# Two feed-forward stages of a three-block forward pass: how the first and last block products are fed

## The chip, the cores and the metric

One core of a Trainium2 chip runs the whole program, from inputs in HBM to outputs in HBM. The metric is the device time of one execution in microseconds (us); the table below gives the median of three runs and a profiled execution.

## The reference

Three blocks with 1024 tokens of width 1024 run one after the other. The change touches the feed-forward part of the second and of the third:

```
# second block
x  = x + mix @ w_out
h2 = rms_norm(x, norm2_g)
x  = x + square(relu(h2 @ w_ff1)) @ w_ff2          # w_ff1 1024 x 4096, w_ff2 4096 x 1024
# third block
x  = x + concatenate([y_conv, y_mla]) @ w_o
hf = rmsnorm(x, norm_ffn_g)
a  = dwconv_centred(hf @ w_up, ffn_conv_w, ffn_conv_b)   # w_up 1024 x 5632, a convolution of 3 along the tokens
g, u = split(a, 2)
x  = x + (silu(g) * u) @ w_down                    # w_down 2816 x 1024
```

## The kernel before

**Tiles.** Activations lie with the channels on the 128 partitions: x[k][hf] is a tile of 128 channels by 512 tokens, k = 0..7, hf = ha or hb, the two halves of the tokens. Every fp32 operand is split by ACT and DVE into a rounded high part and the rest (hi by a cast on ACT, lo by a subtraction on DVE), and mm3 (L286, L287, L288) multiplies hi x hi, lo x hi and hi x lo, so that one 128 x 128 weight block against 512 tokens costs three matmuls.

**Block products.** Both stages save multiplications by Strassen's scheme in Winograd's form. blocks_of_input makes from the tokens the blocks 11, 21, 22 (in ffn3 also 12) and sums T1..T4 of them, each as four hi/lo pairs; some live in the pool tag S, the others in 24 tiles of tag E ("xe"). blocks_of_weights loads two rows of weights (wr), makes four sums S1..S4 in a tile "ss" (L372 to L375 on DVE), and split_w (L309 on ACT, L310 on DVE) makes four hi/lo weight sets, which live in a ring of 3 sets (wb) and nw more (wx; nw is 2 in ffn2 and 1 in ffn3). block_gemm runs seven products of 12 matmuls on them: 11, S1, S2, 12 x 21, S3, S4 and 22 x T4, and adds partial sums kept by ACT (L414) at the evictions. ffn2 has 16 such pairs, the first of them in another form (first_gemm, 9 products). ffn3 has 11 x 2, and the first two of these are plain products of 24 matmuls per half and part.

**ffn2** runs out_part (the output projection, which updates x) for ha, then for hb; each half is normed (squares, inverse_rms), split and spilled to DRAM (xf). The result of a pair goes through relu, a multiply with the norm's factor and a square (L1206, L1207), is summed into blocks again (L1214 to L1217) and stored to DRAM (hd). **ffn3** scales x in place (L1269), splits (L1259, L1260), runs the plain products, then a convolution (L1859 to L1861), a gate (L1286 to L1288) and the sums (L1295 to L1298), and stores.

**block_down** multiplies hd by the second weights in two groups of rows. It loads hidden blocks (hr, L1380) two at a time into a raw ring of two tiles, weight rows r1 (L1386) and r2 (L1394), and the spilled tokens x (L1231, L1361). It takes the seven sets in the order 11, 21, T1, T2, 22, T3, T4, makes the weight sums rs on the way, casts weight blocks to wph and wpl (L1438, L1439), and adds finished sets into x (L1448).

**Order.** Each engine runs its instructions in the order of a list that a scheduler makes when the kernel is built: it takes what is ready by a priority that follows the order of the code, and behind(by) puts a stretch of code that much later in it. Loads are all issued by SP and queue on one hardware queue over 16 DMA engines.

## Time and profile before

| | us |
|---|---|
| median of 3 runs (lowest to highest) | 3149.54 (3147.87 to 3151.3) |
| profiled execution, its own time | 3149.7 |
| its span, from the first to the last instruction | 3147.5 |
| TensorE busy in it | 3023.7 (96%) |
| VectorE (DVE) busy | 2329.6 (74%) |
| ScalarE (ACT) busy | 1419.5 (45%) |
| GpSimd (POOL) busy | 258.7 (8%) |
| mean granted TensorE clock | 0.984 |

The 2.2 us between span and time lie around the instructions. A matmul of 512 columns is recorded with some 0.39 us, but they overlap, so the rate is read from the number that start in a window. The granted clock is given as a share of full speed, 2.4 GHz; a stretch at the lower level, 1.2 GHz, has 0.5.

### The profile page before, as it was taken

The numbers are of one execution on the slowest core, as the hardware profiler recorded it, in microseconds if no ns is written. First come the engines' busy times: TensorE is split into PE (matmuls) and PEld (weight loads), VectorE is DVE, ScalarE is ACT, GpSimd is POOL, SyncE is SP. The second block draws the span as 40 slices with busy tenths as digits, with TensorE's granted clock in tenths as the row PEclk, the third lists the DMA queues.
The fourth block names the chain that finished last, engine by engine and source line by source line (L and its number), as shares of the span: only waits on it lengthen the run. The fifth ranks groups of instructions, "written<-read, shape, count | busy, mean of one in ns | idle before, by whom it ended". The sixth has DMA issues, their size and how long they took to land.

```text
span 3147.5 us, 40045 instructions
## 1 busy us (share of the span) xinstructions
PE 3023.7 (96%) x14472; PEld 2458.8 (78%) x14472; DVE 2329.6 (74%) x3633; ACT 1419.5 (45%) x2258; POOL 258.7 (8%) x352
## 2 busy tenths in 40 slices
PE   8999999999888999999899999999998999999998
PEld 6787888777666777888788888777776888878877
DVE  7756784858688888777867645577778888897776
ACT  3253463323366655444434443265644554454453
POOL 0011011213252000000000022000000000000000
PEclk9999999999999999999999999999999999999999
DMA  4241433423564334444743346642131323365232
GB/s 148 64 124 54 134 123 105 114 61 83 166 161 127 107 116 154 150 151 152 269 166 109 125 119 184 192 134 66 46 131 71 104 101 107 101 212 172 101 104 101
DMA packets 210751, 394.02 MB, mean 125 GB/s; under 512 B 31637, under 2 KB 71957, under 8 KB 210426
## 3 DMA queue, kind: packets, MB, share of 16 engines
q1 hardware_dynamic: 210554, 391.47, 39.5%
q8 instruction: 114, 1.87, 0.2%
q14 instruction: 83, 0.68, 0.1%
HBM read 272.78 MB, written 114.87 MB: 123 GB/s over the span
## 4 chain that ended last, share of the span: by engine, by line
PE 70%; DVE 8%; ACT 2%; issue 2%; DMA 2%; POOL 1%; SPq 0%; POOLq 0%; DVEq 0%; ACTq 0%
PE ps_G L286 12%; PE ps_G L287 12%; PE ps_G L288 12%; PE ps_g L286 4%; PE ps_g L287 4%; PE ps_g L288 4%; PE ps_o L1032 2%; PE ps_o L1033 2%; PE ps_t L2173 2%; PE ps_t L287 1%; PE ps_t L288 1%; PE ps_t L286 1%; PE ps_s L1645 1%; DVE se L1684 1%; PE ps_o L286 1%
## 5 line engine op out<-in xcount | busy, mean ns | idle before, releaser
L286 PE MATMUL ps_G<-xsh,wh 128*128 128x512 f32 (+1 forms) x1004 | 392.9, 391 | 19.0 <-ACT wh L309 11.1
L287 PE MATMUL ps_G<-xsl,wh 128*128 128x512 f32 (+1 forms) x1004 | 390.9, 390 | 1.6 <-DVE xsl L485 1.6
L288 PE MATMUL ps_G<-xsh,wl 128*128 128x512 f32 (+1 forms) x1004 | 390.7, 389 | 0.5 <-DVE wl L281 0.5
L280 ACT CAST wh<-wr 128x1024 fp32r<-128x1024 f32 (+1 forms) x147 | 150.1, 1022 | 272.9 <-PE ps_G L287 77.7
L286 PEld LDWEIGHTS ps_G<-xsh,wh 128*128 128x128 f32 x1004 | 190.2, 189 | 57.9 <-ACT wh L309 11.5
L281 DVE TENSOR_TENSOR wl<-wr,wh 128x1024 fp32r<-128x1024 f32 (+1 forms) x147 | 176.7, 1204 | 78.1 <-ACT wh L280 77.4
L287 PEld LDWEIGHTS ps_G<-xsl,wh 128*128 128x128 f32 x1004 | 189.8, 189 | 39.9 <-DVE xsl L485 2.8
L288 PEld LDWEIGHTS ps_G<-xsh,wl 128*128 128x128 f32 x1004 | 189.8, 189 | 39.1 <-DVE wl L281 1.2
L1031 DVE TENSOR_TENSOR ptl<-ps_t,pth 128x512 fp32r<-128x512 f32 (+3 forms) x288 | 168.6, 617 | 61.7 <-ACT pth L1030 60.2
L1030 ACT CAST pth<-ps_t 128x512 fp32r<-128x512 f32 (+3 forms) x288 | 142.7, 536 | 140.1 <-PE ps_t L2173 73.2
L286 PE MATMUL ps_g<-xsh,wh 128*128 128x512 f32 (+1 forms) x484 | 192.1, 397 | 3.0 <-DVE fa L1206 3.0
L287 PE MATMUL ps_g<-xsl,wh 128*128 128x512 f32 (+1 forms) x484 | 190.6, 394 | 0.3 <-DVE xsl L485 0.2
L288 PE MATMUL ps_g<-xsh,wl 128*128 128x512 f32 (+1 forms) x484 | 190.3, 393 | 0.0
L286 PE MATMUL ps_G<-xe,wh 128*128 128x512 f32 x448 | 176.2, 394 | 4.6 <-ACT xe L330 2.5
L287 PE MATMUL ps_G<-xe,wh 128*128 128x512 f32 x448 | 175.8, 392 | 0.1
L288 PE MATMUL ps_G<-xe,wl 128*128 128x512 f32 x448 | 175.5, 392 | 0.0
L286 PE MATMUL ps_G<-wh,wph 128*128 128x512 f32 x432 | 168.2, 389 | 0.7 <-ACT fz L1345 0.7
L287 PE MATMUL ps_G<-wl,wph 128*128 128x512 f32 x432 | 168.1, 389 | 0.0
L288 PE MATMUL ps_G<-wh,wpl 128*128 128x512 f32 x432 | 168.1, 389 | 0.0
L309 ACT CAST wh<-ss 128x1024 fp32r<-128x1024 f32 x70 | 73.4, 1050 | 151.2 <-PE ps_G L287 107.4
L310 DVE TENSOR_TENSOR wl<-hr,wh 128x1024 fp32r<-128x1024 f32 (+1 forms) x98 | 115.6, 1183 | 17.6 <-ACT wh L309 17.6
L1032 PE MATMUL ps_o<-pth,vst 128*128 128x512 f32 (+3 forms) x288 | 120.0, 417 | 8.8 <-ACT pth L1030 2.9
(618 smaller groups left out, 7603.7 us busy)
## 6 DMA issues: line engine op xcount, KB each, us to landing
wr<-in_w_in_dram SPq DMA_DIRECT2D x65, 512.0 KB
wr<-in_w_up_dram SPq DMA_DIRECT2D x44, 512.0 KB
wr<-in_w_ff_dram SPq DMA_DIRECT2D x33, 512.0 KB
r<-in_w_ff_dram SPq DMA_DIRECT2D x32, 512.0 KB
hr<-hT SPq DMA_DIRECT2D x32, 512.0 KB
h<-fa SPq DMA_DIRECT2D x48, 256.0 KB
hT<-ft SPq DMA_DIRECT2D x48, 256.0 KB
hr<-h SPq DMA_DIRECT2D x24, 512.0 KB
```

The lines of the kernel that those rows point to most:

```text
L280: nc.scalar.copy(hi[:, :n], raw[:, :n])
L281: nc.vector.tensor_tensor(lo[:, :n], raw[:, :n], hi[:, :n].bitcast(F32), op=ALU.subtract)
L286: mm(out, sh, mh, start=start, stop=False, **kw)
L287: mm(out, sh, ml, start=False, stop=False, **kw)
L288: mm(out, sl, mh, start=False, stop=stop, **kw)
L309: self.nc.scalar.copy(hi[:, c], z)
L310: self.nc.vector.tensor_tensor(lo[:, c], z, hi[:, c].bitcast(F32), op=ALU.subtract)
L1030: nc.scalar.copy(hi[:, c0:], tp[:, c0:])
L1031: nc.vector.tensor_tensor(lo[:, c0:], tp[:, c0:], hi[:, c0:].bitcast(F32), op=ALU.subtract)
L1032: nc.tensor.matmul(po[:, c0:], vs, hi[:, c0:], start=start, stop=False)
L1033: nc.tensor.matmul(po[:, c0:], vs, lo[:, c0:], start=False, stop=stop)
L2173: nc.tensor.transpose(tp[:, j * P:(j + 1) * P], pps[j][:, s * P:(s + 1) * P], self.ident)
```

## The change

- **blocks_of_input** is one function for both stages. It spills a half, norms it, scales the tokens in place (ffn2 by a multiply on ACT, ffn3 as before on DVE) and splits them in the order UPPER, then makes the sums T1..T4 in the place of the tokens (16 DVE additions) and splits these; block 12 is split as well. soon names T4 blocks that are split early. out_part goes through its output tiles in the order UPPER.
- **ffn2** computes its first two pairs with plain products (plain_gemm, 24 matmuls for each half and row of blocks) in place of first_gemm; the tiles fa move to a pool of their own, 13 instead of 8, and nw is 1 instead of 2.
- **The weight sums ss** lie in the pool fp, over rows of x that are freed when x is closed.
- **block_gemm** can take the product 12 x 21 second (early), which the first block pair of either stage does. The remaining T parts and the sums of the two plain pairs stand in behind(60), and in ffn3 also the finish of the second plain pair.
- **block_down** loads of the missing r1 rows two at once, into the tile of the weight sums (rr), and the rest, then x, then r2 two at a time between the loads of hr.

Cut to its core:

```diff
+UPPER = (4, 5, 6, 7, 0, 1, 2, 3)
...
-    def blocks_of_input(self, pool, extra, x, gain, a, b):
+    def blocks_of_input(self, pe, x, xf, nm, ha, hb, scale, soon=()):
...
+        B = {n: [None] * 4 for n in ("11", "12", "21", "22", "T1", "T2", "T3", "T4")}
+        new = lambda dt=F32: pe.tile([P, HF], dt, tag="E", bufs=24, name="xe")
+        def parts(n, k, hf):
+            src = x[k][hf]
+            hi, lo = (self.h("xs" + c, "S", F32R) for c in "hl") if n in ("11", "21", "22", "T1") else (new(F32R), new(F32R))
+            A.copy(hi, src)
+            V.tensor_tensor(lo, src, hi.bitcast(F32), op=ALU.subtract)
+            B[n][k % 4] = (hi, lo)
+        for hf, names in ((ha, ("11", "21")), (hb, ("12", "22"))):
+            self.spill(x, xf, hf)
+            _, nm.cols[hf] = self.inverse_rms(self.squares(new, [x[k][hf] for k in UPPER]), D, tag="n", bank="o")
+            for k in UPPER:
+                scale(k, hf)
+                parts(names[k // 4], k, hf)
+            yield B
         for k in range(4):
+            x11, x12, x21, x22 = x[k][ha], x[k][hb], x[k + 4][ha], x[k + 4][hb]
+            V.tensor_tensor(x22, x22, x12, op=ALU.subtract)
+            V.tensor_tensor(x12, x12, x11, op=ALU.subtract)
+            V.tensor_tensor(x11, x22, x11, op=ALU.add)
+            V.tensor_tensor(x21, x21, x11, op=ALU.subtract)
+        yield B
         for k in range(4):
+            parts("T1", k, hb)
+        for k in range(4):
+            parts("T2", k, ha)
+        for k in soon:
+            parts("T4", k, ha)
         yield B
+        for k in range(4, 8):
+            parts("T3", k, hb)
+        for k in range(4, 8):
+            if k not in soon:
+                parts("T4", k, ha)
         yield B
...
-    def blocks_of_weights(self, src1, src2, s):
...
+    def blocks_of_weights(self, src1, src2, pool):
...
-        s1, s2, s4, s3 = s if isinstance(s, list) else [s[:, i] for i in range(4)]
...
+        s = pool.tile([P, 4, HF], F32, tag="ss", bufs=1, name="ss")
+        V.tensor_tensor(s[:, 0], r2[:, lo], r2[:, hi], op=ALU.add)
+        V.tensor_tensor(s[:, 1], s[:, 0], r1[:, lo], op=ALU.subtract)
+        V.tensor_tensor(s[:, 2], r1[:, hi], s[:, 1], op=ALU.subtract)
+        V.tensor_tensor(s[:, 3], r1[:, lo], r2[:, lo], op=ALU.subtract)
+        f = s.rearrange("p n c -> p (n c)")
+        w1, w2, w3, w4 = (self.split_w(z) for z in (r1, f[:, :2 * HF], f[:, 2 * HF:], r2[:, hi]))
         cut = lambda w, c: (w[0][:, c], w[1][:, c])
         return {"11": cut(w1, lo), "12": cut(w1, hi), "22": w4, "S1": cut(w2, lo), "S2": cut(w2, hi), "S4": cut(w3, lo), "S3": cut(w3, hi)}
...
-    def block_gemm(self, pool, w, B, out):
...
+    def block_gemm(self, pool, w, B, out, early=False):
...
+        def first():
+            b = self.pt("g")
+            mul(b, w["12"], B["21"], True, True)
+            out("11", b, p1)
...
+        if early:
+            first()
...
-        u2 = self.keep(pool, "ku2", a)
-        b = self.pt("g")
-        mul(b, w["12"], B["21"], True, True)
-        out("11", b, p1)
+        u2 = keep(a, "ku2")
+        if not early:
+            first()
...
-    def first_gemm(self, w, B):
...
+    def plain_gemm(self, w, B, ha, hf, evict):
+        ps = self.pt("G")
+        self.block_product(ps, w, B["11"] + B["21"] if hf == ha else B["12"] + B["22"], True, True)
+        evict(ps)
...
-        with self.phase("f2", 2, G=4), tc.tile_pool(name="fe", bufs=1, reuse_waits="tile") as pe:
...
+        with self.phase("f2", 1, G=4), tc.tile_pool(name="fe", bufs=1, reuse_waits="tile") as pe, tc.tile_pool(name="fa", bufs=1, reuse_waits="tile") as pa:
+            def act(hf, ps, t=None):
+                z = pa.tile([P, HF], F32, tag="fa", bufs=13, name="fa")
+                if t is not None:
+                    V.tensor_tensor(z, ps, t, op=ALU.add)
+                V.scalar_tensor_tensor(z, ps if t is None else z, 0.0, nm.rst[hf], op0=ALU.max, op1=ALU.mult)
+                A.activation(z, z, AF.Square)
+                return z
...
+            def hidden(p, h):
...
+                V.tensor_tensor(h["12"], h["12"], h["11"], op=ALU.subtract)
+                V.tensor_tensor(t4, h["21"], t2, op=ALU.subtract)
+                for n, z in (("11", h["11"]), ("T1", h["12"]), ("21", h["21"]), ("T2", t2), ("22", h["22"]), ("T3", t3), ("T4", t4)):
+                    nc.sync.dma_start(hd[n][p], z)
+            steps = self.blocks_of_input(pe, x2, xf, nm, ha, hb, lambda k, hf: A.mul(x2[k][hf], x2[k][hf], self.v("norm2_g", k)))
...
+            def plain(p, hf):
+                for r in range(2):
+                    def ev(ps):
+                        h[p][f"{r + 1}{1 if hf == ha else 2}"] = act(hf, ps)
+                    self.plain_gemm(wts[p][r], B, ha, hf, ev)
+            for _ in self.out_part(w, xd, yt, x2, (5, 6, 7), (ha,)):
+                pass
+            B = next(steps)
+            for _ in self.out_part(w, xd, yt, x2, (5, 6, 7), (hb,)):
+                pass
+            wts = [[self.load_w(d["w_ff1"][p + 16 * r]) for r in range(2)] for p in range(2)]
+            plain(0, ha)
+            next(steps)
+            next(steps)
+            plain(0, hb)
+            plain(1, ha)
+            plain(1, hb)
+            next(steps)
+            with self.behind(60):
+                hidden(0, h[0])
                 next(steps)
+                hidden(1, h[1])
             self.close_x()
             self.fpool = tc.tile_pool(name="fp", bufs=1, side="right", reuse_waits="tile")
...
-                        wts = self.blocks_of_weights(d["w_ff1"][p], d["w_ff1"][p + 16], pf.tile([P, 4, HF], F32, tag="ss", bufs=1, name="ss"))
+                for p in range(2, 16):
+                    wts = self.blocks_of_weights(d["w_ff1"][p], d["w_ff1"][p + 16], fp)
...
-                        self.block_gemm(pf, wts, B, act)
...
+                    def out(n, ps, t):
+                        h[n] = act(ha if n[1] == "1" else hb, ps, t)
+                    self.block_gemm(pf, wts, B, out, p == 2)
+                    hidden(p, h)
...
+            def scale(k, hf):
+                V.scalar_tensor_tensor(x[k][hf], x[k][hf], self.v("norm_ffn_g", k), nm.rst[hf], op0=ALU.mult, op1=ALU.mult)
+            steps = self.blocks_of_input(pe, x, xf, nm, ha, hb, scale, (7,))
...
+            def plain(j, hf):
+                for part in range(2):
+                    self.plain_gemm(wts[j][part], B, ha, hf, lambda ps: A.copy(z[j][part][:, zs(hf)], ps))
...
-            split_half(ha, ("11", "21"))
+            B = next(steps)
...
-            for part in range(2):
-                plain(wts[0][part], ha, z[0][part])
-            split_half(hb, ("12", "22"))
...
+            plain(0, ha)
+            next(steps)
+            next(steps)
+            plain(0, hb)
+            h = [finish(0, z[0]), None]
...
-                for part in range(2):
-                    plain(wts[1][part], hf, z[1][part])
-            h[1] = finish(nf, z[1])
-            for n, o, hf in (("T1", 0, hb), ("T2", 0, ha), ("T3", 4, hb), ("T4", 4, ha)):
-                for k in range(4):
...
+            plain(1, ha)
+            plain(1, hb)
+            next(steps)
+            with self.behind(60):
+                next(steps)
+                h[1] = finish(nf, z[1])
...
-                        wts = self.blocks_of_weights(d["w_up"][f], d["w_up"][22 + f], p2.tile([P, 4, HF], F32, tag="ss", bufs=1, name="ss"))
+                        wts = self.blocks_of_weights(d["w_up"][f], d["w_up"][22 + f], fp)
...
-                        self.block_gemm(p2, wts, B, out)
+                        self.block_gemm(p2, wts, B, out, f == 1)
+                        if f == 1:
+                            with self.behind(60):
+                                blocks(0, *h, p2)
...
-                    blocks(i, *h, p2)
+                    if i:
+                        blocks(i, *h, p2)
...
+            def load_r1(kk):
+                for k in kk:
+                    o = ks.index(k)
+                    if o < nfp:
+                        r1[k] = fp.tile([P, 2 * HF], F32, tag="r1", bufs=nfp, name="r1")
+                    elif o == nfp:
+                        both = fp.tile([P, 4, HF], F32, tag="ss", bufs=1, name="rr").rearrange("p n c -> p (n c)")
+                        r1[k] = both[:, :2 * HF]
+                        if o + 1 < len(ks):
+                            r1[ks[o + 1]] = both[:, 2 * HF:]
+                    elif o > nfp + 1:
+                        r1[k] = pd.tile([P, 2 * HF], F32, tag="r1", bufs=nb - nfp - 2, name="r1")
+                    nc.sync.dma_start(r1[k], rows(k))
...
-            for o, k in enumerate(ks):
-                if k not in r1:
-                    r1[k] = (fp if o < nb // 2 else pd).tile([P, 2 * HF], F32, tag="r1", bufs=nb // 2, name="r1")
-                    nc.sync.dma_start(r1[k], rows(k))
+            need = [k for k in ks if k not in r1]
+            two = [ks[j:j + 2] for j in range(0, len(ks), 2)]
+            n1 = 2 if load_x is not None else len(need)
+            load_r1(need[:n1])
...
-                load_x(0, ha)
...
+                later += [lambda: load_r1(need[n1:]), lambda f=load_x: f(0, ha)]
+            later += [lambda kk=kk: load_r2(kk) for kk in two]
...
-        for n in range(KT):
+        for n in UPPER:
```

Three places of the order, first before, then after (the lines are those of each kernel). DVE at the start of ffn3, when the second half's tokens are scaled: vn ends the norm, x is scaled by the norm's factor rst, xe and xsl are the low parts; x_18165, x_18515, x_18871, x_19221 are tiles 0 to 3 before, and x_18128, x_18478, x_18834, x_19184, x_19540 are tiles 4, 5, 6, 7 and 0 after.

```order
L507 TENSOR_SCALAR vn_21252<-ps_o_21247 128x4
L1269 SCALAR_TENSOR_TENSOR x_18165<-x_18165,vc_70,rst_21256 128x512
L1269 SCALAR_TENSOR_TENSOR x_18515<-x_18515,vc_70,rst_21256 128x512
L1269 SCALAR_TENSOR_TENSOR x_18871<-x_18871,vc_70,rst_21256 128x512
L1260 TENSOR_TENSOR xe_21265<-x_18165,xe_21264 128x512
L1269 SCALAR_TENSOR_TENSOR x_19221<-x_19221,vc_70,rst_21256 128x512
L1260 TENSOR_TENSOR xe_21270<-x_18515,xe_21269 128x512
```

```order
L489 TENSOR_SCALAR vn_21215<-ps_o_21210 128x4
L1244 SCALAR_TENSOR_TENSOR x_18128<-x_18128,vc_70,rst_21219 128x512
L1244 SCALAR_TENSOR_TENSOR x_18478<-x_18478,vc_70,rst_21219 128x512
L1244 SCALAR_TENSOR_TENSOR x_18834<-x_18834,vc_70,rst_21219 128x512
L327 TENSOR_TENSOR xsl_21228<-x_18128,xsh_21227 128x512
L1244 SCALAR_TENSOR_TENSOR x_19184<-x_19184,vc_70,rst_21219 128x512
L327 TENSOR_TENSOR xsl_21233<-x_18478,xsh_21232 128x512
L1244 SCALAR_TENSOR_TENSOR x_19540<-x_19540,vc_70,rst_21219 128x512
```

Tile 0, the first of block 12, was scaled first and is now scaled fifth.

DVE before the first block pair of ffn3: fc, fth and ft belong to the convolution, the gate and the block sums of the plain pairs, xe to the T parts, ss are the weight sums.

```order
L1287 SCALAR_TENSOR_TENSOR fth_21509<-fth_21509,fc_21497 128x512
L1260 TENSOR_TENSOR xe_21562<-x_19579,xe_21561 128x512
L1288 SCALAR_TENSOR_TENSOR fc_21501<-fth_21509,fc_21501 128x512
L1260 TENSOR_TENSOR xe_21566<-x_19929,xe_21565 128x512
L1260 TENSOR_TENSOR xe_21570<-x_20285,xe_21569 128x512
L1260 TENSOR_TENSOR xe_21574<-x_20674,xe_21573 128x512
L1295 TENSOR_TENSOR ft_21584<-fc_21501,fc_21381 128x512
L372 TENSOR_TENSOR ss_21598<-wr_21600 128x512
L1296 TENSOR_TENSOR ft_21585<-ft_21584,fc_21381 128x512
L1297 TENSOR_TENSOR fc_21381<-fc_21381 128x512
L1298 TENSOR_TENSOR ft_21586<-fc_21501,ft_21585 128x512
L373 TENSOR_TENSOR ss_21598<-ss_21598,wr_21599 128x512
```

```order
L1841 SCALAR_TENSOR_TENSOR fc_21524<-fz_21350,vc_70,fc_21524 128x1024
L327 TENSOR_TENSOR xe_21513<-x_18130,xe_21512 128x512
L1842 SCALAR_TENSOR_TENSOR fc_21524<-fz_21350,vc_70,fc_21524 128x1024
L327 TENSOR_TENSOR xe_21517<-x_18480,xe_21516 128x512
L308 TENSOR_TENSOR wl_21569<-wr_21548,wh_21568 128x512
L327 TENSOR_TENSOR xe_21521<-x_18836,xe_21520 128x512
L366 TENSOR_TENSOR ss_21551<-wr_21548 128x512
L369 TENSOR_TENSOR ss_21551<-wr_21547,wr_21548 128x512
L367 TENSOR_TENSOR ss_21551<-ss_21551,wr_21547 128x512
L1841 SCALAR_TENSOR_TENSOR fc_21528<-fz_21353,vc_70,fc_21528 128x1024
L368 TENSOR_TENSOR ss_21551<-wr_21547,ss_21551 128x512
```

The gate and the block sums that stood between the T parts and the second weight sum are gone from there, and the weight sums follow the T parts.

SP at the step from ffn2's pairs to its down product: h and hT are stores of the hidden blocks, r are weight rows (L1386 and L1362 for r1, L1394 and L1367 for r2), x the spilled tokens, hr the hidden blocks.

```order
L1386 DMA r_13665<-in_w_ff_dram 128x1024
L1231 DMA x<-xf 128x512 x4
L1394 DMA r_13679<-in_w_ff_dram 128x1024
L1394 DMA r_13682<-in_w_ff_dram 128x1024
L1394 DMA r_13721<-in_w_ff_dram 128x1024
L1394 DMA r_13724<-in_w_ff_dram 128x1024
L1394 DMA r_13765<-in_w_ff_dram 128x1024
L1394 DMA r_13768<-in_w_ff_dram 128x1024
L1394 DMA r_13809<-in_w_ff_dram 128x1024
L1394 DMA r_13812<-in_w_ff_dram 128x1024
L1380 DMA hr<-h_10761 128x2x512
L1231 DMA x<-xf 128x512 x4
```

```order
L1362 DMA r_13633<-in_w_ff_dram 128x1024
L1367 DMA r_13717<-in_w_ff_dram 128x1024
L1221 DMA x<-xf 128x512 x4
L1367 DMA r_13720<-in_w_ff_dram 128x1024
L1367 DMA r_13761<-in_w_ff_dram 128x1024
L1367 DMA r_13764<-in_w_ff_dram 128x1024
L1347 DMA hr<-h_10761 128x2x512
L1367 DMA r_13813<-in_w_ff_dram 128x1024
L1367 DMA r_13816<-in_w_ff_dram 128x1024
L1347 DMA hr<-h_10761 128x2x512
L1367 DMA r_13857<-in_w_ff_dram 128x1024
L1367 DMA r_13860<-in_w_ff_dram 128x1024
```

The first hr of block 21 stood behind eight r2 loads and stands behind four now, and x between the first two of them.

## Rows read from the trace of the kernel before

**Rows 1.** TensorE, 100 us: width, busy (starts) by engine, clock, DMA share, GB/s.

```profile
1500.00:1600.00 100.00, 89.16 (x382) 72.77 (x381) 76.87 (x110) 42.84 (x62) 0.00 (x0) 0.93 0.67 236
...
2600.00:2700.00 100.00, 100.00 (x443) 82.81 (x442) 89.17 (x110) 50.51 (x64) 1.27 (x20) 1.00 0.32 106
```

**Rows 2.** TensorE's waits over the execution: total us, times, longest.

```profile
PE ps_g L286 <- ACT wh L309: 15.1, 2, 8.9
...
PE ps_G L286 <- ACT wh L309: 11.1, 1, 11.1
...
PE ps_g L286 <- DVE fa L1206: 3.0, 1, 3.0
...
PE ps_G L286 <- ACT xe L330: 2.5, 1, 2.5
...
PE ps_g L287 <- DVE wl L310: 2.4, 2, 1.9
...
PE ps_G L286 <- ACT xe L1259: 2.1, 1, 2.1
...
PE ps_o L522 <- POOL un L510: 1.5, 2, 1.3
```

**Rows 3.** Short windows around the waits, columns as in rows 1.

```profile
1192.00:1208.00 16.00, 10.30 (x30) 6.82 (x29) 15.32 (x24) 8.68 (x15) 0.00 (x0) 0.68 0.53 180
1512.00:1532.00 20.00, 9.16 (x29) 6.57 (x28) 20.00 (x33) 12.07 (x19) 0.00 (x0) 0.66 0.96 352
2360.00:2372.00 12.00, 8.55 (x37) 6.81 (x36) 7.58 (x13) 4.89 (x8) 1.01 (x1) 0.86 0.00 0
2404.00:2424.00 20.00, 8.91 (x31) 6.73 (x31) 18.68 (x28) 8.16 (x13) 0.13 (x2) 0.74 0.59 210
2820.00:2836.00 16.00, 9.39 (x32) 6.82 (x31) 15.84 (x25) 10.11 (x16) 0.00 (x0) 0.79 0.73 266
```

**Rows 4.** ACT and DVE at ffn2's start: start, us, engine, line, operation.

```profile
1195.41 3.26 ACT L330 CAST xe<-bt 128x512 fp32r<-128x512 f32 x6 [3.31 <-DVE bt L354]
...
1197.94 2.49 DVE L331 TENSOR_TENSOR xe<-bt,xe 128x512 fp32r<-128x512 f32 x4
1200.35 0.68 DVE L1206 SCALAR_TENSOR_TENSOR fa<-ps_g,rst 128x512 f32<-128x512 f32 x1
```

**Rows 5.** Timeline of SP, ACT, DVE from ffn2 to down; one window.

```profile
1503.07 6.90 SPq L1394 DMA_DIRECT2D r<-in_w_ff_dram  x8
1510.92 0.38 SPq L1380 DMA_DIRECT2D hr<-h  x1
...
1521.48 1.04 ACT L309 CAST wh<-hr 128x1024 fp32r<-128x1024 f32 x1
...
1513.48 2.47 DVE L1448 TENSOR_TENSOR x<-x,ps_G 128x512 f32<-128x512 f32 x4
...
1508.00:1516.00 8.00, 5.68 (x26) 4.36 (x24) 5.37 (x10) 2.48 (x4) 0.00 (x0) 1.00 1.03 412
```

**Rows 6.** Timeline of ACT at ffn3's start.

```profile
2365.37 1.94 ACT L1259 CAST xe<-x 128x512 fp32r<-128x512 f32 x3 [0.82 <-DVE x L1269]
...
2369.22 0.62 ACT L1259 CAST xsh<-x 128x512 fp32r<-128x512 f32 x1 [0.64 <-DVE x L1269]
```

**Rows 7.** Timeline of DVE, ACT, TensorE before ffn3's first block pair.

```profile
2405.08 1.28 DVE L1861 SCALAR_TENSOR_TENSOR fc<-fz,vc,fc 128x1024 f32<-128x1024 f32 x1
...
2415.31 0.68 DVE L373 TENSOR_TENSOR ss<-ss,wr 128x512 f32<-128x512 f32 x1
...
2416.03 1.04 ACT L309 CAST wh<-ss 128x1024 fp32r<-128x1024 f32 x1 [5.25 <-DVE ss L373]
...
2417.12 0.80 PE L286 MATMUL ps_G<-xsh,wh 128*128 128x512 f32 x1 [11.09 <-ACT wh L309]
```

**Rows 8.** Timeline of SP and ACT from ffn3 to down.

```profile
2820.87 0.37 SPq L1380 DMA_DIRECT2D hr<-g  x1
...
2827.96 1.04 ACT L309 CAST wh<-hr 128x1024 fp32r<-128x1024 f32 x1 [2.73 <-DMA hr<-g]
```

196 lines of the change are left out of this document (33 added, 163 removed).

## The prediction

> **What bounds the kernel now.** First the table of 100 us windows [rows 1]. In an undisturbed stretch (2600-2700) TensorE is busy 100% at granted clock 1.00 and starts 443 matmuls in 100 us, 0.2257 us each; the window 1500-1600 has 89.16% and 382. TensorE's issue is the bound, so time is to be gained only where it stands still or runs at the lower clock. Then TensorE's waits over the whole execution [rows 2], of which seven are in the diff's reach, and short windows around them [rows 3]. A window's loss is its width less its matmuls times 0.2257: start of ffn2 16 - 30 x 0.2257 = 9.2 us (A); from ffn2's pairs to its down product 20 - 6.5 = 13.5 (B); first block pair of ffn3 20 - 7.0 = 13.0 (C); from ffn3's pairs to its down product 16 - 7.2 = 8.8 (D). At the start of ffn3 (C0) the window also holds twelve short matmuls of the norm, so I add instead: waits of 1.3 (POOL's un) and 2.1 us (xe, L1259), and 12 x 0.14 x 2 = 3.4 us at half clock, of which half is lost: 5.1 us. Together **49.6 us**: no fix of these five places can bring more, so 3149.7 - 49.6 = 3100.1 us is the floor.
>
> The two levels are 1.2 and 2.4 GHz, so clock means of 0.68, 0.66, 0.86, 0.74 and 0.79 [rows 3] are 10.2 + 13.6 + 3.4 + 10.4 + 6.7 = 44.3 us at the lower. The waits themselves are 5.5 + 10.8 + 3.4 + 11.1 + 6.6 = 37.4 us [rows 2], so the clock costs 49.6 - 37.4 = 12.2. The Trainium skill (TensorE: Matmul & The Clock Gate, section HAM oscillation) reckons the loss as half of the throttled time, here an estimate of 22.2 us, and 59.6 in all. The trace does not agree: TensorE stood still for much of the throttled time, and the counts of matmuls leave 12.2. By that rule the sum below would grow by 59.6/49.6 (rival 6).
>
> **No work is added for TensorE.** ffn2 had 9 products of 12 matmuls in its first pair and 15 x 7 after: 114. Two plain pairs are 2 x 8, and 14 x 7 remain: 114. ffn3 keeps its two plain pairs. Each edit therefore moves only what TensorE waits for.
>
> **A, start of ffn2.** Before, the scaled T sums are made while TensorE is already at the products that need them: ACT's casts of the parts wait 3.31 us for a sum (L354) and begin at 1195.41, DVE makes the last four low parts from 1197.94, and only then the eviction L1206 at 1200.35, for which TensorE waits [rows 4]. That piece gives the unit costs too: 0.6 us for a DVE part (four in 2.49), 0.54 for an ACT cast (six in 3.26). After, the two plain pairs need only parts of 11, 21, 12, 22: 192 matmuls x 0.2257 = 43.3 us of cover. Under it DVE has 8 low parts of hb, 16 in-place sums, 16 T parts, 4 weight sums (44 x 0.6 = 26.4), 8 evictions (5.4) and 4 weight splits (4.8): 37 us. ACT has 16 multiplies or casts of hb, 16 T casts, 8 + 8 squares (48 x 0.6 = 29) and 4 weight casts (4.2): 33 us. Both fit, DVE by 6 us. The order puts the T4 parts, which need the E tiles of 12 free, and the first weight sums behind the fourth eviction pair; the cast of S1, S2 then follows TensorE's last read of 12 by some 2.7 + 4 x 0.6 us, and TensorE needs it two products (5.4 us) after the plain pairs. Where the multiply in place waits for its spill to land, ACT holds all casts behind it; a slip of the whole 9.2 us is needed to lose it all. Gain **9.2**, bounds 4 and 9.2: DVE 5 us over its cover leaves 5. The weight ring falls from 5 sets to 4; ffn3 has run with 4 before, at 100% in 2600-2700 [rows 1], so it is costed at nothing.
>
> **C0, start of ffn3.** The tokens are now scaled 4..7, 0..3, so 12's first block, which TensorE's first matmul of plain(0, hb) needs, is the fifth instead of the first. Before, the first cast begins at 2365.37 and the fifth at 2369.22 [rows 6]: **3.85 us** later. The stand-still grows from 2.1 to 6.0 us, and with it, I take it, the stretch at half clock from 3.4 to 6.8 us, 1.7 more. Cost 3.9 to 5.6.
>
> **C, first block pair of ffn3.** Before, DVE reaches L373 at 2415.31, ACT's cast follows at 2416.03, TensorE goes on at 2417.12 [rows 7] and pays 13.0 - 11.1 = 1.9 us more for the low clock, as if it went on at full speed from 2419.0. In the order of before 25 DVE rows follow the 1024-wide split of wr up to and with L373; after, 16. Two convolution steps (1.2 each: L1861), four gate steps and four output sums (8 x 0.6) less, one more weight sum: 6.6 us, and up to 1.8 us of waits between them. Thus L373's end falls from 2416.0 to 2407.6-2409.4, the cast ends a microsecond later, at 2408.6-2410.5. TensorE itself, which ran out of work at 2417.12 - 11.09 = 2406.0 and is moved by C0, arrives at 2409.9-2411.6. So it hardly waits, and C0 and C together gain 2419.0 - 2410.7 = 8.3; 0.8 off for the split of the lows: **7.5**, bounds 4 (a wait of 3 us is left, and its clock) and 10.4 (C0 costs nothing; then DVE is the bound, 2419.0 - 2408.6). The 6.6 us of DVE work moved behind must fit into the block pair that follows (7 x 12 x 0.2257 = 19 us); only the pairs' stores to hd wait for it.
>
> **B, ffn2 to down.** Before, the loads of r2 (8 x 0.524 MB) are issued from 1503.07, hr of block 21 behind them at 1510.92, and its cast begins at 1521.48; the engines move 412 GB/s there [rows 5]: they are full, and the queue's order decides. After, four r2 stand behind hr and two r1 go out before the last stores, into free time: 6 x 0.524 / 0.412 = 7.6 us earlier, the cast at 1513.9, and ACT has four r2 casts fewer ahead of it. TensorE is due at 1521.48 + 1.1 - 8.9 = 1513.7. The two early r1 go into the weight-sum tile and wait on SP until pair 15's splits have read it, with three hr of 11 and the pair's stores queued behind them; those hr are needed before 1513.7 as well, but 11 was fed without a wait before. But the low part (DVE, 1.2 us) now stands behind the additions into x, which wait for product 11 to end and take 2.47 for four [rows 5]; one of them is ahead: 0.6 + 1.2 us. I take a wait of 1.8 and 1.7 of clock: gain 13.5 - 3.5 = **10**, bounds 6 (hr 4 us later) and 13.5.
>
> **D, ffn3 to down.** hr of 21 goes from behind twelve x loads (12 x 0.262 MB = 3.1 MB) to before them: 3.1 / 0.412 = 7.6 us, cast at 2827.96 - 7.6 = 2820.4 [rows 8], due at 2827.96 + 1.1 - 6.2 = 2822.9. Hidden. The x loads land later by one hr (1.3 us), and x is added to at the end of 11, with the low part behind it on DVE: gain **8.5**, bounds 5 and 8.8. Behind these DMAs the SP queue holds the next hr alone, which waits for a ring slot anyhow.
>
> The second group of either down product, and the end phase, keep their loads; a few matmuls trade places: 0, bounds -3 and +3.
>
> **Sum.** 9.2 + 7.5 + 10 + 8.5 = 35.2 us off the profiled execution of 3149.7 us (span 3147.5 and 2.2 around it), which is 0.2 over the median of the runs. **3114.5 us.**
>
> **Rivals.** (1) *The loads stay late*: with the engines full, stores and x compete with hr and B and D bring half. For it: 412 GB/s at 1508-1516 [rows 5]. Against: In 1500-1600 the queue alone delays hr. B 5, D 4: 3124. (2) *The backlog moves*: DVE is over its cover in A (5 left) and C keeps 5: 3125. For it: DVE was at the parts until 1200.35 [rows 4]. (3) *Everything goes*: UPPER costs nothing, the low part of B is in time: 9.2 + 10.4 + 13.5 + 8.8 = 41.9, 3108. Against: the scale waits for the norm, which comes at the same time. (4) *Slower, by the weight ring of ffn2*: with 4 sets a pair's last set is recast only after the pair before has read it; if that cast and split (1.05 + 1.2 us) stood once in each of 14 pairs, with 1.7 of clock, it is 4 x 14 = 56 us: 3114.5 + 56 = 3170. It outweighs the gain from 35.2 / 14 = 2.5 us a pair. Against: ffn3 at 100% with the same ring [rows 1]. (5) *It doesn't do what it says*: hr, S1 and the plain pairs wait nearly as long for what stands next in line (x additions, E tiles, spills), and 5 us of the 35 remain: 3145. (6) *The clock gives back more than its rows*: half of the 44.3 us, so 35.2 x 59.6 / 49.6 = 42: 3107.
>
> **How the numbers follow.** Forecast 0.48, (1) 0.18, (2) 0.15, (3) 0.05, (6) 0.02, (5) 0.06, (4) 0.06. A measurement here tells 0.2%, 6.3 us, from no change: faster below 3143.2. Faster 0.88, same 0.06, slower 0.06. The forecast's own bounds are about 3108 and 3122. The range leaves out (4) and (5), reaches below (3) and (6), and above (1) and (2) to where both come half together: 3104 to 3132.
>
> **What would show it.** Right: no wait on L1206 or xe at ffn2's start; TensorE's wait on the first xe of ffn3 near 6 us instead of 2.1; L309's waits of 11.1, 8.9 and 6.2 gone or under 2; the windows of 1500-1600 and 2800-2900 at 98% or more; 14 pairs of ffn2 at 100%. Wrong: waits on wh or wl in each pair of ffn2 (4); a wait on hr's cast above 4 us (1); DVE without idle and TensorE waiting on ss or xe (2).

## The result and the profile after

The changed kernel takes 3115.46 us (median of four runs, 3111.93 to 3118.55) against 3148.70 (3147.56 to 3151.30) for the kernel before beside it: ratio 0.9893, interval 0.9881 to 0.9906. The forecast was 3114.5, with a range of 3104 to 3132. The profiled execution took 3116.86 us, with a span of 3115.1; the span of before is 3147.5.

The 32.4 us between the spans (33.2 between the medians; 35.2 were forecast) can be laid to stretches, by cutting both traces at the same instructions: the first matmul of ffn2's down product, the norm's column sums behind it, those at the start of ffn3, the first matmul of ffn3's down product, and its end.

| stretch | before | after | gained | forecast |
|---|---|---|---|---|
| start to ffn2's down product (A) | 1491.73 | 1487.79 | 3.94 | 9.2 |
| ffn2's down product to the norm (B) | 318.56 | 305.15 | 13.41 | 10 |
| attention | 520.83 | 519.56 | 1.27 | 0 |
| start of ffn3 to its down product (C0, C) | 464.25 | 457.40 | 6.85 | 7.5 |
| ffn3's down product (D) | 218.16 | 209.96 | 8.20 | 8.5 |
| end | 134.01 | 135.21 | -1.20 | 0 |

So the sum came out within 2.8 us, C and D did, and two terms missed in opposite directions: A by 5.3 us, B by 3.4.

The windows of 100 us, in the columns of [rows 1]: ffn2's start, its pairs, its step to down, and the end of ffn3's step to down, which now begins at 2769.90.

```profile
1100.00:1200.00 100.00, 94.40 (x443) 75.33 (x442) 77.03 (x124) 59.15 (x101) 8.41 (x2) 0.98 0.36 112
...
1300.00:1400.00 100.00, 100.00 (x443) 82.87 (x442) 68.57 (x98) 40.48 (x57) 0.00 (x0) 1.00 0.47 161
...
1500.00:1600.00 100.00, 99.78 (x440) 82.35 (x439) 84.44 (x123) 46.20 (x67) 0.00 (x0) 1.00 0.73 257
...
2800.00:2900.00 100.00, 99.30 (x439) 82.03 (x438) 84.90 (x122) 44.41 (x64) 0.00 (x0) 1.00 0.49 162
```

The window that began at 1500 stood at 89.16% and 382 matmuls [rows 1]; it is full now. The pairs of ffn2 run at 443 matmuls in 100 us with four sets of weights: rival 4 is refuted by that row. TensorE's waits, as [rows 2] (total, times, longest), of the places in the diff's reach:

```profile
PE ps_G L287 <- ACT xe L326: 6.0, 1, 6.0
PE ps_o L504 <- POOL un L492: 4.5, 3, 3.0
...
PE ps_g L287 <- DVE x L1429: 0.7, 1, 0.7
PE ps_G L289 <- DVE wl L308: 0.6, 1, 0.6
```

The line that was L309 (the cast of a weight, 15.1 and 11.1 us) is L307 now and is not among the waits at all; nor is the eviction fa. The wait on the first xe of ffn3 is 6.0 us in the place of 2.1, as forecast. What was not forecast is the second line: un, which cost 1.5 us in all, costs 4.5, with one wait of 3.0. Both are seen in short windows, columns as before:

```profile
1184.00:1200.00 16.00, 13.04 (x53) 10.40 (x52) 11.00 (x20) 5.49 (x9) 7.40 (x1) 0.89 0.04 16
...
2340.00:2360.00 20.00, 12.52 (x51) 9.54 (x50) 14.22 (x24) 7.37 (x12) 1.01 (x1) 0.74 0.02 8
```

**A, the new wait.** POOL is busy for 7.40 us with one instruction of 128x4 in the first window. The timelines of POOL, DVE and TensorE there (start, length, engine, line; x are the in-place sums):

```profile
1184.23 7.40 POOL L492 TENSOR_TENSOR un<-vn,nhalf 128x4 f32<-128x4 f32 x1 [23.61 <-DVE vn L489]
...
1183.99 0.15 DVE L489 TENSOR_SCALAR vn<-ps_o 128x4 f32<-128x4 f32 x1
1184.06 0.69 DVE L339 TENSOR_TENSOR x<-x 128x512 f32<-128x512 f32 x1
...
1190.08 0.69 DVE L340 TENSOR_TENSOR x<-x 128x512 f32<-128x512 f32 x1
...
1191.69 0.73 PE L504 MATMUL ps_o<-cn,un 128*128 128x128 f32 x4 [2.96 <-POOL un L492]
```

vn is there at 1184.14; un begins at once and ends at 1191.63, 0.86 us after the last of the in-place sums with which the change fills DVE. TensorE, which needs un for the norm's rows, stands still for 2.96 us, and the granted clock of the window is 0.89: 16 x 0.11 x 2 = 3.5 us at the lower level behind it. In the kernel before, the same instruction took 1.38 us:

```profile
1175.77 1.38 POOL L510 TENSOR_TENSOR un<-vn,nhalf 128x4 f32<-128x4 f32 x1 [16.43 <-DVE vn L507]
```

**B.** ACT and DVE at the step to down, the rows that answer to [rows 5]:

```profile
1507.79 1.05 ACT L307 CAST wh<-hr 128x1024 fp32r<-128x1024 f32 x1 [0.80 <-DMA hr<-h]
...
1507.71 0.69 DVE L1429 TENSOR_TENSOR x<-x,ps_G 128x512 f32<-128x512 f32 x1
1508.87 1.23 DVE L308 TENSOR_TENSOR wl<-hr,wh 128x1024 fp32r<-128x1024 f32 x1 [0.48 <-ACT wh L307]
```

Counted from the down product's first matmul, the cast of block 21 comes at 20.0 us in the place of 29.75: 9.75 us earlier, where 7.6 were forecast. Only one addition into x stands ahead of the low part, and it was over by then; the forecast wait of 1.8 us is not there, only 0.22 us for the low part itself.

**C and D.** Of the first block pair of ffn3, DVE's sum, ACT's cast and TensorE (compare [rows 7]):

```profile
2390.00 0.68 DVE L367 TENSOR_TENSOR ss<-ss,wr 128x512 f32<-128x512 f32 x1
...
2390.72 1.05 ACT L307 CAST wh<-ss 128x1024 fp32r<-128x1024 f32 x1 [0.43 <-DVE ss L367]
...
2393.68 0.50 PE L289 MATMUL ps_G<-xsh,wl 128*128 128x512 f32 x1 [0.61 <-DVE wl L308]
```

The cast ends at 2391.77 and TensorE comes to it at 2392.0, without a wait where 11.09 us stood; 0.61 is left for the low part. In D the cast of block 21's last rows, the one that TensorE waited for before, comes 2791.73 - 2769.90 = 21.8 us behind the first matmul, in the place of 32.6 [rows 8]: 10.8 us earlier, where 7.6 were forecast. Behind it 0.70 us of waits remain, for an addition into x:

```profile
2791.73 1.04 ACT L307 CAST wh<-hr 128x1024 fp32r<-128x1024 f32 x1
...
2803.53 0.47 PE L287 MATMUL ps_g<-wh,wph 128*128 128x512 f32 x1 [0.70 <-DVE x L1429]
```

### The profile page after: what moved, and what is told of

Same layout as the page of the kernel before. It is cut to its first block, busy times and chain, and to the rows that moved or that the text cites. A ratio compares the mean times of both kernels' runs of the same rounds, so it can differ in the third digit from the quotient of the medians.

```text
span 3115.1 us, 39929 instructions
## 1 busy us (share of the span) xinstructions
PE 3018.5 (97%) x14472; PEld 2457.3 (79%) x14472; DVE 2310.0 (74%) x3618; ACT 1420.2 (46%) x2263; POOL 264.4 (8%) x352
## 4 chain that ended last, share of the span: by engine, by line
PE 70%; DVE 8%; issue 2%; ACT 2%; DMA 2%; POOL 1%; SPq 0%; POOLq 0%; DVEq 0%; ACTq 0%
PE ps_G L287 12%; PE ps_G L288 12%; PE ps_G L289 12%; PE ps_g L287 4%; PE ps_g L288 4%; PE ps_g L289 4%; PE ps_o L1014 2%; PE ps_o L1015 2%; PE ps_t L2154 2%; PE ps_t L287 1%; PE ps_t L289 1%; DVE se L1665 1%; PE ps_t L288 1%; PE ps_s L1626 1%; PE ps_o L287 1%
## 5 line engine op out<-in xcount | busy, mean ns | idle before, releaser
L287 PE MATMUL ps_G<-xsh,wh 128*128 128x512 f32 (+1 forms) x1024 | 400.8, 391 | 8.3 <-ACT xsh L462 6.4
L288 PE MATMUL ps_G<-xsl,wh 128*128 128x512 f32 (+1 forms) x1024 | 399.1, 390 | 1.0 <-DVE xsl L467 1.0
L289 PE MATMUL ps_G<-xsh,wl 128*128 128x512 f32 (+1 forms) x1024 | 398.8, 390 | 1.1 <-DVE wl L308 0.6
L282 DVE TENSOR_TENSOR wl<-wr,wh 128x1024 fp32r<-128x1024 f32 (+1 forms) x151 | 181.0, 1202 | 75.0 <-ACT wh L281 74.2
L307 ACT CAST wh<-hr 128x1024 fp32r<-128x1024 f32 (+1 forms) x98 | 99.8, 1018 | 65.4 <-PE ps_G L289 19.4
L307 ACT CAST wh<-ss 128x1024 fp32r<-128x1024 f32 x68 | 71.3, 1049 | 126.1 <-PE ps_G L288 82.5
```

The costliest lines, as they stand in the source:

```text
L282: nc.vector.tensor_tensor(lo[:, :n], raw[:, :n], hi[:, :n].bitcast(F32), op=ALU.subtract)
L287: mm(out, sh, mh, start=start, stop=False, **kw)
L288: mm(out, sh, ml, start=False, stop=False, **kw)
L289: mm(out, sl, mh, start=False, stop=stop, **kw)
L307: self.nc.scalar.copy(hi, src)
```

## The experiments

Each is one edit of the changed kernel. "Stage C" is the stretch from the start of ffn3 to its down product, 457.40 us in the changed kernel.

**e1_natural: ffn3 scales and splits rows 0..7 again.**

```diff
-            for k in UPPER:
+            for k in order if hf == hb else UPPER:   # order = range(KT) in ffn3
```

> The changed kernel, but ffn3 scales and splits the second half's tokens in the order 0..7 again. Theory (DVE bounds the stretch from this norm to the first S1 product of ffn3, so the late start costs nothing): TensorE's wait on the first xe falls from 6.0 to about 2.1 us, and a wait of 6 to 12 us comes back before S1; the time stays at 3114 to 3121 us. Rival (the order UPPER is a plain cost of 3.85 us and its clock): the time falls by 7 us to about 3108, with no wait before S1.

3122.55 us (3119.38 to 3124.99), ratio 0.9916 (0.9901 to 0.9931). The wait on xe falls to 2.11 us, and a wait for S1 of 8.90 comes back; TensorE and ACT:

```profile
2397.17 0.79 PE L287 MATMUL ps_G<-xsh,wh 128*128 128x512 f32 x1 [8.90 <-ACT wh L307]
...
2396.07 1.04 ACT L307 CAST wh<-ss 128x1024 fp32r<-128x1024 f32 x1 [3.28 <-DVE ss L367]
```

Stage C takes 462.39 us, 5.0 longer. The rival, that the early start is a pure gain (3108), is false. The run is less clean than it was meant to be: with the rows in this order the scheduler also put more of DVE's convolution and gate steps ahead of the weight sums, so S1's cast comes 5.0 us later from the stage's start. Counted from the stage's start, TensorE comes to S1 at 75.44 us in the place of 79.50, and in the changed kernel the cast ends at 79.27; so even without that delay an estimate of 3.8 us of wait would be left. The 3.9 us won at the start are worth nothing unless DVE reaches the sums sooner; UPPER by itself is not priced. The time is 1.6 us above the theory's range, which did not reckon with the moved steps.

**e2_loads_old: the down products load in the order of before** (the tiles and the two early rows of r1 kept).

```diff
-            load_r1(need[:n1])
+            load_r1(need)
...
-                later += [lambda: load_r1(need[n1:]), lambda f=load_x: f(0, ha)]
+                load_x(0, ha)
```

> The changed kernel, but the down products queue their loads as before: all missing r1 rows, then x, then r2 two at a time from the first hr on; the tiles are those of the change, so two r1 rows still go into the weight-sum tile. Theory (the queue's order sets when hr of block 21 lands): that hr is again behind eight r2 loads or behind x, TensorE waits 5 to 9 us at the first product of 21 in ffn2's down and 4 to 6 in ffn3's, and with the clock the time rises by 14 to 21 us, to 3130-3137. Rival (the two early r1 rows alone did it): it rises by under 5 us.

3131.54 us (3129.37 to 3134.69), ratio 0.9946 (0.9931 to 0.9961). TensorE's waits:

```profile
PE ps_g L287 <- ACT wh L307: 5.0, 2, 4.3
...
PE ps_g L288 <- DVE wl L308: 3.3, 2, 2.3
```

B is 8.7 us longer and D 4.3: of the 21.6 us that both gained, the place in SP's queue is worth 13.0 in this trace and 16 in the medians. In B the first cast of block 21 is this one:

```profile
1513.99 1.04 ACT L307 CAST wh<-hr 128x1024 fp32r<-128x1024 f32 x1 [0.30 <-DMA hr<-h]
```

It comes 25.1 us behind the down product's first matmul (1488.90), against 20.0 in the changed kernel and 29.75 before. The four r2 loads that are ahead of it again should take 4 x 0.524 / 0.412 = 5.1 us, and it is 5.1 us later; a match as close as that is chance, for e6 below, with the changed kernel's own order, has this cast 1.2 us later. The other 4.7 us come with what this edit keeps, the tiles and the early rows; neither was tested by itself. In ffn3 the edit does not bring back the order of before: the last hr of block 21 still goes ahead of x, and the waits, 3.1 us where 4 to 6 were expected, are those for T1, whose hr stands behind sixteen loads of x.

**e3_sums_behind: the in-place sums of ffn2 get a lower priority.**

```diff
-            next(steps)
+            with self.behind(40):
+                next(steps)
```

> The changed kernel, but the sixteen in-place sums of ffn2 are put behind the second half's norm in the order. Theory (GpSimd's un, 7.40 us in the changed kernel and 1.38 before, is held while DVE runs these sums back to back): un takes 1.0 to 1.7 us, the wait of 2.96 us on it goes, with 3.4 us at half clock: 4 to 5 us less, 3110 to 3112. Rival (un is late because vn is queued on DVE behind an eviction): un stays above 4 us, or the wait stays above 1.5.

3114.19 us (3112.00 to 3120.59), ratio 0.9894 (0.9879 to 0.9908). Inconclusive: the scheduler hardly moved the sums, and un was still held, for 6.80 us, with a wait of 2.56 on TensorE. But the granted clock stayed at 1.00 behind this wait:

```profile
1183.26 6.80 POOL L492 TENSOR_TENSOR un<-vn,nhalf 128x4 f32<-128x4 f32 x1 [23.80 <-DVE vn L489]
...
1183.00:1199.00 16.00, 13.44 (x62) 10.84 (x61) 13.20 (x23) 7.46 (x13) 6.80 (x1) 1.00 0.07 28
```

From the norm's column sums to the down product this kernel takes 327.6 us, the changed one 329.5.

**e4_finish_first: in ffn3 the convolution and gate of the second block, the last parts and the block sums stand in their old place.**

```diff
-            with self.behind(60):
-                next(steps)
-                h[1] = finish(nf, z[1])
+            h[1] = finish(nf, z[1])
+            next(steps)
...
-                            with self.behind(60):
-                                blocks(0, *h, p2)
+                            blocks(0, *h, p2)
```

> The changed kernel, but in ffn3 the finish of the second plain pair, the last T parts and the block sums of the plain pairs stand in their old place ahead of the first block pair. Theory (DVE's backlog ahead of the second weight sum is what C was): TensorE waits 5 to 8 us before S1 and loses 1.7 more by the clock: 3121 to 3125. Rival (moving 12 x 21 ahead of S1 hides it alone): a wait of under 2 us, 3115 to 3118.

3124.35 us (3120.41 to 3127.50), ratio 0.9921 (0.9905 to 0.9938). TensorE at S1:

```profile
2398.49 0.50 PE L287 MATMUL ps_G<-xsh,wh 128*128 128x512 f32 x1 [3.26 <-ACT wh L307]
...
2400.95 0.79 PE L289 MATMUL ps_G<-xsh,wl 128*128 128x512 f32 x1 [1.27 <-DVE wl L308]
```

Stage C is 463.63 us, and 464.25 in the kernel before: with DVE's steps in their old place nearly all of C's gain is gone. The waits are 4.5 us, 3.26 of them for S1 where 5 to 8 were expected, and the granted clock of 2392 to 2408 is 0.79. The rival, that the product of part 12 with 21 hides the wait alone, is out: that product stands ahead of S1 here as well.

**e5_pause: DVE stands still while un is computed.** After the first four sums of ffn2 a copy of four columns of un is put on DVE, and the other twelve sums are queued behind it.

```diff
+                if k == 1 and not soon:
+                    t = self.small("brk", (P, 4), bufs=1)
+                    cx.enter_context(self.tc.issue_after(V.tensor_copy(t, nm.cols[hb][:, :4]).ins))
```

> One edit against the changed kernel: at the start of ffn2, VectorE does the first 4 of the 16 in-place sums, then a copy of 4 columns of un (so it stands still until GpSimd has computed un), then the other 12 sums. In the changed kernel un took 7.40 us while VectorE ran the 16 sums without a pause and ended 0.86 us after the last of them; it took 1.38 us in the kernel before, where no such sums ran beside it. Theory (the row of sums holds GpSimd up for as long as it runs): un now takes 1.0 to 1.8 us, the wait of TensorE for un (2.96 us) is gone and with it the 3.4 us at the low clock behind it (1.7 us lost), VectorE loses about 2 us, which are covered: 3111 to 3113 us against 3115.5. Rival (un is late for another reason, such as vn coming 1.3 us late on VectorE): un still takes 5 us or more, or TensorE waits as long for it, and the time stays within 3 us of 3115.5 or goes above it.

3113.86 us (3110.76 to 3115.84), ratio 0.9883 (0.9868 to 0.9898). POOL and DVE there, and then the window:

```profile
1185.32 1.39 POOL L496 TENSOR_TENSOR un<-vn,nhalf 128x4 f32<-128x4 f32 x1 [24.90 <-DVE vn L493]
...
1186.74 0.17 DVE L340 COPY brk<-un 128x4 f32<-128x4 f32 x1 [0.90 <-POOL un L496]
```

```profile
1184.00:1200.00 16.00, 16.00 (x76) 13.29 (x76) 15.10 (x27) 8.32 (x15) 1.39 (x1) 1.00 0.09 34
```

un takes 1.39 us, the window is full at clock 1.00, and DVE paid 0.90 us of idle time for it. From the norm's column sums to the down product it takes 326.40 us, against 329.5 to 331.2 in the seven kernels in which un took 7.4 us (the changed one, e1, e2, e4, e6, e7, e9). So the row of sums is what held un; that vn came late is not the cause. Held, it cost A 3.1 us or more in those seven, and 1.2 in e3, where the clock did not fall. This is the fastest kernel here by its median, 0.9 us above the theory's 3111 to 3113, but its interval overlaps that of the changed one: the times alone don't tell the two apart.

**e6_rows_late: no early rows of r1 ahead of block 21.**

```diff
-            n1 = 2 if load_x is not None else len(need)
+            n1 = 0 if load_x is not None else len(need)
```

> One edit against the changed kernel: in block_down none of the remaining loads of the first rows of the residual goes ahead of the weights' high-low part (n1 = 0 in the place of 2), so that part stands behind two more loads of about 1.25 us each on SP's queue. In the changed kernel its cast came 1.76 us before it was due at the step from ffn2 to down. Theory (the place in the queue decides, and what is left is slack of 1.8 us): the part comes 2.5 us later, TensorE waits about 0.7 us, at most with a stretch at the low clock behind it: 3115 to 3120 us. Rival (the early tiles, not the queue, gave the gain of this step): no wait at all, and 3115.5 within 2 us. If the wait is over 3 us, the slack was read wrongly: 3121 to 3125.

3115.02 us (3112.50 to 3121.57), ratio 0.9889 (0.9867 to 0.9911). The edit changed nothing: the rows that it takes from the first call are loaded by the next step of the code, and SP's queue and every engine run the same instructions in the same order as in the changed kernel. So this is the changed kernel measured a second time, and neither the theory nor the rival was tested. TensorE at the low part of block 21:

```profile
1510.04 0.51 PE L287 MATMUL ps_g<-wh,wph 128*128 128x512 f32 x1 [0.35 <-ACT wh L307]
...
1511.30 0.51 PE L288 MATMUL ps_g<-wl,wph 128*128 128x512 f32 x1 [0.76 <-DVE wl L308]
```

The waits of 1.1 us here and of 0.22 in the other trace are what two executions of one order differ by. The slack of 1.8 us was counted to the start of the cast, whose 1.05 us belong to it: some 0.7 were left.

**e7_no_swap and e9_s1_first: the product of part 12 with 21 in its old place.**

```diff
-                    self.block_gemm(pf, wts, B, out, p == 2)
+                    self.block_gemm(pf, wts, B, out)
...
-                        self.block_gemm(p2, wts, B, out, f == 1)
+                        self.block_gemm(p2, wts, B, out)
```

> One edit against the changed kernel: the first group of block products after the first half takes its plain pairs in the old order (the product of part 12 with 21 in its old place, early = False) in both ffn stages. S1 is then wanted 2.73 us earlier. In the changed kernel S1's cast in ffn3 came 0.2 us before TensorE wanted it, in ffn2 4.7 us before. Theory: in ffn2 no wait; in ffn3 a wait of about 2.5 us and some 3.4 us at the low clock behind it (1.7 us lost): 3118 to 3121 us. Rival (VectorE's row of work sets the end of this stage whatever TensorE waits for, so the wait only moves): 3115.5 within 2 us.

3116.86 us (3114.95 to 3117.57), ratio 0.9892 (0.9877 to 0.9907), and no wait for S1 in either stage. For ffn2 that is the theory. Its 3118 to 3121 was for a wait in ffn3 that did not come about: there the edit changes nothing that bears on S1: the scheduler issues what is ready first, and the product stayed ahead of S1 although the code names it later. It did so in the kernel before, too. These are the first and the last of its 12 matmuls (ps_g) there, and behind them TensorE waited 11.09 us for S1 [rows 7]:

```profile
2403.15 0.39 PE L286 MATMUL ps_g<-xsh,wh 128*128 128x512 f32 x1
...
2405.65 0.39 PE L288 MATMUL ps_g<-xsh,wl 128*128 128x512 f32 x1
```

So taking this product second gave ffn3 an order on TensorE that it already had, and is no part of C's gain. In e9 it is tied behind the last matmul with S2, an order that neither kernel has:

```diff
         if not early:
-            first()
+            with (self.tc.issue_after(self.lm.ins) if early is None else ExitStack()): first()
```

> As e7, but in ffn3 TensorE is bound to do the products with S1 and S2 first and the product of part 12 with 21 behind them (in e7 the scheduler kept that product ahead, since its data were there sooner, so ffn3 stayed as in the changed kernel). S1 is then wanted 2.73 us earlier than in the changed kernel, where its cast came 0.2 us before TensorE came to it. Theory (the early product covers the time in which VectorE makes the sums of the weights): TensorE waits about 2.5 us for S1's cast in ffn3, at most with a stretch of 3.4 us at the low clock behind it (1.7 us lost), nothing in ffn2: 3117 to 3120 us. Rival (VectorE sets the end of this stage, so the wait only moves): the same wait, but the stage from the start of ffn3 to down as long as before within 1 us: 3115.5 within 2 us.

3120.44 us (3119.23 to 3121.72), ratio 0.9908 (0.9891 to 0.9924). TensorE and ACT at S1, and then the window:

```profile
2394.34 0.50 PE L287 MATMUL ps_G<-xsh,wh 128*128 128x512 f32 x1 [2.38 <-ACT wh L307]
...
2393.24 1.05 ACT L307 CAST wh<-ss 128x1024 fp32r<-128x1024 f32 x1 [0.43 <-DVE ss L367]
```

```profile
2388.00:2404.00 16.00, 12.98 (x49) 9.99 (x48) 14.73 (x21) 8.50 (x12) 0.25 (x4) 0.89 0.54 181
```

A wait of 2.38 us, 0.11 x 16 x 2 = 3.5 us at the lower level, and stage C at 461.14, 3.7 us longer: the theory (its 3117 to 3120 missed by 0.4), and the rival that the wait only moves is out. The product ahead of S1 covers DVE's sums, and losing it costs 3.7 us; but the kernel before had it there too, so none of C's 6.85 us comes from it.

**e8_beside and e10_beside2: un beside rows of DVE, measured alone.** Short pieces ahead of the kernel: DVE makes a vn of four columns, POOL computes un from it, and meanwhile DVE does 12 operations of 128x512 of one form.

> The changed kernel with six short pieces ahead of its first load; its output isn't touched. In each piece VectorE makes a vn of 4 columns, GpSimd computes un from it by the same operation as in the norm, and meanwhile VectorE does 12 operations of 128x512 without a pause, of another form in each piece: 0, tensor_scalar of one tile in SBUF; 1, tensor_tensor of a bank in PSUM and a tile in SBUF; 2, tensor_tensor of two tiles in SBUF; 3, the same in place; 4, scalar_tensor_tensor of two tiles in SBUF; 5, tensor_tensor of two tiles in SBUF into a rounded tile. Theory (an operation of VectorE with two operands in SBUF keeps GpSimd's operation waiting): un takes 1.0 to 1.8 us in pieces 0 and 1, and 5 us or more, until the 12 end, in 2 to 5. Rival (any full row on VectorE does that): 5 us or more in all six. Rival (none does; un was late for another reason): 1.0 to 2.0 us in all six. The program's time is longer by the pieces, some 40 to 60 us, and says nothing else.

un in the six pieces, POOL's timeline:

```profile
6.05 1.19 POOL L2180 TENSOR_TENSOR pru<-prv,nhalf 128x4 f32<-128x4 f32 x1 [4.25 <-DVE prv L2179]
11.38 1.01 POOL L2180 TENSOR_TENSOR pru<-prv,nhalf 128x4 f32<-128x4 f32 x1 [4.14 <-DVE prv L2179]
20.97 8.01 POOL L2180 TENSOR_TENSOR pru<-prv,nhalf 128x4 f32<-128x4 f32 x1 [8.58 <-DVE prv L2179]
29.47 1.38 POOL L2180 TENSOR_TENSOR pru<-prv,nhalf 128x4 f32<-128x4 f32 x1 [0.49 <-DVE prv L2179]
37.16 1.38 POOL L2180 TENSOR_TENSOR pru<-prv,nhalf 128x4 f32<-128x4 f32 x1 [6.30 <-DVE prv L2179]
44.86 1.38 POOL L2180 TENSOR_TENSOR pru<-prv,nhalf 128x4 f32<-128x4 f32 x1 [6.32 <-DVE prv L2179]
```

Half of the theory holds: neither piece with one operand in SBUF held un up, and one with two did, for 8.01 us, to the end of DVE's row. But three others with two operands took 1.38. Twelve more pieces were to tell what decides.

> As e8, with twelve pieces: three times over the same four, in this order: with an operation of 128x1024 with two operands in SBUF right ahead of vn, then 12 times tensor_tensor of two tiles into another (a) or in place (b); without that wide operation, the same two (c, d). In e8 one of the four streams with two operands in SBUF held GpSimd's un up (8.01 us, to the end of the stream), the three others didn't (1.38 us). Theory 1 (what goes right ahead on VectorE decides, since the piece that was held up followed such a wide operation): un 7 us or more in all a and b, 1.0 to 1.8 us in all c and d. Theory 2 (in place or not decides): 7 us or more in a and c alone. Theory 3 (it is a matter of chance at the moment at which the two meet): 7 us or more in some and not in others, without order. The program's time is longer by the pieces, some 100 us, and says nothing else.

All twelve in one row, minimum, median and maximum in ns:

```profile
L2181 POOL TENSOR_TENSOR pru<-prv,nhalf x12: 1307/1378/8007, 8.8 to 101.0; 128x4 f32<-128x4 f32 x12
```

Only the third, the first c, took 8.01 us; its twin pieces took 1.38. Theory 2 is refuted, and theory 1 for the wide operation of the pieces: none of the six a and b was held. But the scheduler put work of the kernel between the pieces, and so a wide operation also ahead of this c, the split of a weight (L282). DVE ahead of the two pieces that were held, first e8, then e10:

```profile
19.60 1.21 DVE L282 TENSOR_TENSOR wl<-wr,wh 128x1024 fp32r<-128x1024 f32 x1
20.73 0.15 DVE L2179 TENSOR_SCALAR prv<-pb 128x4 f32<-128x4 f32 x1
...
25.64 1.21 DVE L282 TENSOR_TENSOR wl<-wr,wh 128x1024 fp32r<-128x1024 f32 x1
26.77 0.16 DVE L2180 TENSOR_SCALAR prv<-pb 128x4 f32<-128x4 f32 x1
```

No other of the 16 pieces with two operands comes right behind that split; they are also the two ahead of which POOL had been idle longest, 8.58 and 8.25 us against at most 7.32. Neither is shown to be the cause: in the changed kernel an eviction of 128x512 goes ahead of vn, and in the kernel before un took 1.38 us after 16.43 of idle time. Theory 3, chance, explains nothing, and what decides whether un is let in stays open.

## Why the prediction came out as it did

**The bound was read rightly.** Each gain and loss that could be placed in these twelve traces is a wait of TensorE, or a stretch at its lower clock behind one.

**A was mis-sized: 9.2 forecast, 3.9 measured**, 5.2 if counted from the norm's column sums (334.76 to 329.54). The 1.3 between them lie ahead of the stage, within what runs differ by there: the column sums begin at 1156.97 before and 1158.25 after, and at 1156.60 in e6, which runs the same order. The waits it named are gone, and DVE had room. The step that failed is the cover: the 37 us of DVE work under two plain pairs were counted against DVE's own time alone, and not against what else is slowed by a row of sums without a gap. The un of ffn2's norm was in no term, since TensorE did not wait for it before (the 1.3 us of [rows 2] are the un of ffn3, and stay); it now costs 2.96 us and a stretch at the lower clock. With the pause of e5 the same stretch gains 334.76 - 326.40 = 8.4 us, near the 9.2.

**B was mis-sized: 10 forecast, 13.4 measured.** The queue argument holds (e2). The step that failed is the residual wait: 1.8 us and 1.7 of clock were taken for the addition into x ahead of the low part, as if it ran when TensorE already stood waiting. It ran at 1507.71, before the cast began, and the cast came 2.1 us earlier than six loads alone would give. Part of those 2.1 is run to run: in e6, the same order, the cast comes at 21.2 us and not at 20.0. The gain is 0.1 short of the bound of 13.5.

**C0 and C: 7.5 forecast, 6.85 measured.** The first xe is waited for 5.97 us, as worked out (6.0). The clock behind it is dearer: mean 0.74 over 20 us, 10.4 us at the lower level where 6.8 were taken. In return S1 is not waited for at all. The waits of C0 and C together fell from 3.4 + 11.1 to 7.5 + 1.0 us, 6.0 of the 6.85. The reckoning holds step by step: counted from the stage's start, the cast ends at 79.3 us where 77.5 to 79.4 were forecast, and TensorE comes to it at 79.5, forecast 78.8 to 80.5. e4 shows that the DVE steps moved behind are what gives the gain.

**D: 8.5 forecast, 8.2 measured**, with 0.7 us left for an addition into x, the one that the prediction named.

**The rest**: attention +1.27 and the end -1.20 add up to nothing, within the 3 us allowed.

**The rivals.** (1) is what e2 looks like; the loads did come in time. (2), a backlog on DVE at 3125, is what e4 looks like (3124.35), but not the changed kernel. (3) fails by the wait on xe, (4) by the windows of ffn2's pairs, (5) by the waits on L307 that are gone. (6): the five short windows of before held some 44.3 us at the lower clock, those of after 13.9, so 30.4 less. The waits in these places fell from 37.4 to 12.0 us, 25.4 less; the 33.7 us gained (with A from the column sums) leave 8.3 for the clock, 0.27 of that time and not half. The prediction's 12.2 of 44.3 is nearly the same share. That A and B missed by 5.3 and 3.4 in opposite directions is luck in the total, and the range had room for either alone. Its upper end does not follow from its own words: half of (1) and half of (2) together give 3124.5, both in full 3134.5, and not 3132.

## What to carry to other kernels

Price moved work not only on its own engine but on those that must get a word in beside it: a tiny instruction of POOL on the critical path can be held for as long as DVE's row lasts, and a pause of 0.9 us was cheaper than the full row here. Where transfers are at their limit, it is the order in the queue that decides, and it is worked out from bytes ahead and rate. Before an edit of the order is trusted or tested, compare the order that the scheduler makes of it with the order that it made before: e3, e6 and, in ffn3, e7 moved little or nothing of what they were to move, and the product that the change names second in ffn3 had run second all along.
